# Two decoder blocks on one core: V products of the expert layer with the weights of the tokens stationary, and 128 tokens served by gathering

## The chip, the core and the metric

The kernel runs on one core of a Trainium2 chip, in one launch. The metric is the device time of one execution in microseconds; the kernel before has a median of 2870.73 us over three runs (2870.41 to 2872.3). All arithmetic is in float32: products are made of three float32r matmuls, since every operand is split into a high part and a low rest (high x high, high x low, low x high).

## The reference, cut to what matters

Two decoder layers over 512 tokens of 1024 channels. The change lies in the feed-forward part of the first one, a layer with 16,384 experts of one hidden unit each, of which every token takes 128 (8 heads, 16 each):

```
s = einsum(q, keys)                      # two sets of 128 key scores per head
sv, si = top_k(s, 16); top_s, sel = top_k(sums of pairs, 16)
eidx = the 128 expert numbers of a token; g = softmax(top_s)
u = u_tab[eidx]                          # rows of 1024
act = gelu(einsum('chkd,cd->chk', u, xb))
w = g * act
out = einsum('chk,chkd->cd', w, v_tab[eidx])
```

## The kernel before, in words

Tokens stand in columns: hT is 128 channels by 8 blocks by 528 tokens. The expert layer treats 416 of the 512 tokens **densely** and the other 96 **by gathering**.

Dense: the experts are cut into 128 chunks of 128. For each chunk `u_chunk` (L905) multiplies the U rows of the chunk with the 416 normed tokens (24 matmuls, `mm_late`, L264) and takes gelu; the result, 128 experts by 416 tokens, is `act`. The routing (`routing`, L1119, a generator that is fed from a budget of DVE time per chunk, `BUD`, L47) turns the top-k results into the dense matrix G of gate weights, 128 experts by tokens for each chunk: one-hot rows on DVE (`onehots`), matmuls and a scaled copy (`build_g`, L1105), 16 tokens at a time, 26 blocks, written to a DRAM buffer `gd`. Of the 128 chunks 84 (`ahead`, L189) have their U products made in the U stage, while DVE routes, and are spilled to DRAM (`ad`); the other 44 ("fresh") are made later, between the V products.

V stage (from L1152): in 16 runs of 8 chunks. `load_g` (L1160) reads a run's G back, in 2 transfers from POOL's queue; `load_a` reads a spilled act; `w_prod` (L1172) multiplies act with G on DVE; `w_split` (L1178) makes `wth` and `wtl`. `v_pass` (L1189) is called twice per run, once per half of the channels. It takes 512 of the 1024 columns of the chunk's V rows as the stationary operand, 4 blocks of 128, and the 416 tokens as the moving one, 24 matmuls per chunk over both halves, and sums the 8 chunks of the run in PSUM; then two DVE instructions (L1206) add the sums to hT.

Gathered: `gathered` (L928) is a generator of steps, `gstep` takes one. A step fetches 128 rows of U, or later of V, by expert number (`indirect_dma_start` from POOL's queue, L935) into one of 3 buffers `row` (GB), two steps ahead of its use, and does one DVE multiply over 128 x 1024: U rows with the token and a sum along the row (L949), V rows scaled and added up (L958). Groups (64 tokens, 2 copies) and (32, 4) make 128 + 64 steps. 26 gathers come ahead of the first read of G, the other 166 in the V stage.

Order: everything is in program order on each engine. V rows (`Stream`, L96) are split into high and low by ACT (L119) and DVE (L121), two pieces ahead; U weights of fresh chunks by ACT and POOL. SP issues the loads. `enter` (L1214) splits hT for the next layer and sums its squares; in the last pass its first four blocks are called between the V products of the second half.

Of the kernel before, what the change touches and what calls it, by code (L numbers as in the profile page):

```python
# [46 lines left out]
BUD = 5.0  # L47
# [12 lines left out]
GROUPS = ((64, 2), (32, 4))  # L60
# [32 lines left out]
GV = (1, 2, 4, 6)  # L93
# [48 lines left out]
def _body(tc, nc, V, S, PE, GP, A, out, upto, tap, ctx):  # L142
    def pool(stack, name, bufs=1, **kw):
        if kw.get("space") != bass.MemoryType.DRAM:
# [11 lines left out]
                 "nsa": NSAP}  # L156
# [619 lines left out]
    with ExitStack() as st:  # L776
        with st0 as st1:
            with ExitStack() as st2:
# [59 lines left out]
                xnh, xnl = xtile(xp)  # L838
# [22 lines left out]
                def norm_x(k):  # L861
                    tn = xq.tile([128, T], F32, name="tn", bufs=2)
                    V.scalar_tensor_tensor(tn, H[k], col("g_ffn", k), rB[:, :T], op0=OP.mult, op1=OP.mult)
                    split(xnh[:, k], xnl[:, k], tn, None)
# [40 lines left out]
            def u_chunk(c, p, bufs=3):  # L905
# [3 lines left out]
                a = p.tile([128, TD], F32, name="act", bufs=bufs)  # L909
                S.activation(a, ps, AF.Gelu)  # L910
                return a
# [16 lines left out]
            def gathered():  # L928
# [4 lines left out]
                def load(a, v, j):  # L933
                    g = gx.tile([128, 1024], F32, name="row", bufs=GB)
# [4 lines left out]
                for t in todo[:GB - 1]:  # L939
                    load(*t)  # L940
                yield
# [29 lines left out]
            gat, gac = [], {}  # L971

# [172 lines left out]
            while live:  # L1145
                try:
# [4 lines left out]

        pk = pool(st, "pk")  # L1152
        vs_ = pool(st, "vs", 4)
        order = [f0 + sp_ + f1 for f0, sp_, f1 in runs]
        order[0] = runs[0][0] + runs[0][2] + runs[0][1]
# [4 lines left out]
        def load_g(r):  # L1160
            if r < len(runs):
                gt[r] = pk.tile([128, NSB, RUN, SUB], F32, name="gt", bufs=2)
                for b in range(0, NSB, NSB // GP_):
                    sl = slice(b, b + NSB // GP_)
                    nc.gpsimd.dma_start(gt[r][:, sl].rearrange("p b i t -> p b (i t)"),
                                        gd[sl, :, RUN * r:RUN * (r + 1)].rearrange("b p i t -> p b (i t)"))

        def load_a(c):
            aw[c] = pk.tile([128, TD], F32, name="act", bufs=6)
            nc.sync.dma_start(aw[c], ad[c])  # L1170

        def w_prod(c):  # L1172
            r = c // RUN
            a = aw[c]
            V.tensor_tensor(a.rearrange("p (b t) -> p b t", t=SUB), a.rearrange("p (b t) -> p b t", t=SUB),
                            gt[r][:, :, c % RUN, :], op=OP.mult)

        def w_split(c):  # L1178
            a = aw.pop(c)
            hi = pk.tile([128, TD], F32R, name="wth", bufs=RUN + 2)  # L1180
            lo = pk.tile([128, TD], F32R, name="wtl", bufs=RUN + 2)
# [3 lines left out]
        def u_fresh(c):  # L1185
            aw[c] = u_chunk(c, pk, 6)
            gstep(GU)

        def v_pass(r, h, steps, after=None):  # L1189
            acc = [bank("d") for _ in range(2)]  # L1190
            for j, c in enumerate(order[r]):
                w = vst.get()
                for d in range(4):
                    mm3(acc[d // 2][:, (d % 2) * 512:(d % 2) * 512 + TD], w, d * 128, nw[c][0], nw[c][1],
                        j == 0, j == RUN - 1)
                for fn, arg in steps.get(j, ()):
                    fn(arg)
                if j in GV:
                    gstep()
                if h == 1:  # L1200
                    nw.pop(c)
            for fn, arg in steps.get(RUN, ()):
                fn(arg)
            for d in range(2):
                k = 4 * h + 2 * d
                V.tensor_tensor(hT[:, k:k + 2, M0:M0 + TD], acc[d].rearrange("p (a t) -> p a t", a=2)[:, :, :TD],  # L1206
                                hT[:, k:k + 2, M0:M0 + TD], op=OP.add)
            if after is not None:
                after(range(4 * h, 4 * h + 4))
# [18 lines left out]
        def skew(seq, ahead_):  # L1228

            st_ = {}  # L1230
            for j, c in enumerate(seq):
                if c is not None:
                    st_.setdefault(j - ahead_, []).insert(0, (w_prod, c))
                    st_.setdefault(j - ahead_ + 1, []).append((w_split, c))
            return st_

        load_g(0)
        f0, sp_, f1 = runs[0]
        early = f0 + f1 + runs[1][0][:PRE]
        nf = len(early)  # L1240
        for i, c in enumerate(early):
            if i == nf - EL:
                for c_ in order[0][:2]:
                    w_prod(c_)
                for c_ in order[0][:2]:
                    w_split(c_)
                vst.pump(3, 1)
            u_fresh(c)
            if i == VP:
                vst.pump(3, -1)  # L1250
        for c in sp_[:6 - nf]:
            load_a(c)
        w_prod(order[0][2])
        steps0 = skew([None, None, None] + order[0][3:], 2)
        steps0[0] = [(w_split, order[0][2])]
        for j, c in enumerate(sp_[6 - nf:]):
            steps0.setdefault(j, []).append((load_a, c))
# [647 lines left out]
```

## Time and profile before

| | |
|---|---|
| median of three runs | 2870.73 us |
| profiled execution | 2870.35 us, span 2868.2 us |
| PE, DVE, ACT, POOL busy | 96, 66, 42, 31% of the span |
| U stage (350 to 850.7 us) | PE busy 472.3, DVE 421.8 us |
| V stage (850.7 to 1615 us) | PE busy 760.0, DVE 577.3 us, DMA 284 GB/s |

The profile is of one execution. Stages are told apart by the lines that run in them; a stage's limit is the engine that nobody keeps waiting there. A matmul's own duration in the trace includes its way through the array and overlaps the next, so rates are read from starts.

### The profile page before, as it was taken

The page shows a single profiled execution, that of the slowest core. Times are in us where ns is not written, and L with a number is a line of the kernel's source. Part 1 is how long each engine was busy: PE and PEld are TensorE (multiplying, and loading weights), DVE is VectorE, ACT ScalarE, POOL GpSimd, SP SyncE. Part 2 cuts the span into 40 slices and gives each one's busy share as a digit, 9 for nine tenths or more (in the row PEclk, how much of TensorE's full clock was granted, in tenths as well). Part 3 has the DMA queues.
Part 4 walks back from the last instruction along what each step waited for, and adds up shares of the span by engine and source line. Part 5 has one row for each costly group of instructions (what it writes and reads, how often), then busy time and mean ns, then how long its engine had stood idle before and what let it go on. Part 6 is the DMA issues. An engine that isn't in the chain of part 4 may idle for free. (4 is left out here: it accounts for less than half of the span.)

```text
span 2868.2 us, 38216 instructions
## 1 busy us (share of the span) xinstructions
PE 2758.8 (96%) x14308; PEld 2429.1 (85%) x14308; DVE 1905.4 (66%) x3477; ACT 1193.5 (42%) x1962; POOL 876.0 (31%) x521
## 2 busy tenths in 40 slices
PE   8778998999999999999999999999999999999998
PEld 7646898999989999999999988888887866788887
DVE  5887599798957867777778765444436489544433
ACT  5564543646553333343333423332223378433322
POOL 3653155555534456564456000000003133000000
PEclk9889999999999999999999999999999999999999
DMA  3102255767678888888888333333234200233332
GB/s 126 52 8 66 70 175 179 262 193 259 211 278 305 285 295 281 306 283 280 294 296 301 99 101 96 96 97 100 91 101 141 81 23 1 74 99 100 96 94 83
DMA packets 156568, 457.17 MB, mean 159 GB/s; under 512 B 17056, under 2 KB 40864, under 8 KB 152800
## 3 DMA queue, kind: packets, MB, share of 16 engines
q1 hardware_dynamic: 103008, 273.33, 29.5%
q0 software_dynamic: 36704, 135.54, 14.2%
q10 hardware_dynamic: 16672, 45.88, 4.0%
q8 instruction: 112, 1.84, 0.3%
q14 instruction: 72, 0.59, 0.1%
HBM read 407.43 MB, written 47.25 MB: 159 GB/s over the span
## 5 line engine op out<-in xcount | busy, mean ns | idle before, releaser
L119 ACT CAST wh<-wr 128x1024 fp32r<-128x1024 f32 (+1 forms) x356 | 369.4, 1038 | 394.4 <-issue 206.3
L121 DVE TENSOR_TENSOR wl<-wr,wh 128x1024 fp32r<-128x1024 f32 (+1 forms) x231 | 287.5, 1245 | 368.1 <-ACT wh L119 363.4
L121 POOL TENSOR_TENSOR wl<-wr,wh 128x1024 fp32r<-128x1024 f32 x125 | 334.0, 2673 | 330.2 <-ACT wh L119 325.4
L262 PE MATMUL m<-xh,wl 128*128 128x512 f32 x1080 | 422.2, 391 | 3.4 <-POOL wl L121 2.7
L260 PE MATMUL m<-xh,wh 128*128 128x512 f32 x1080 | 424.4, 393 | 0.0
L261 PE MATMUL m<-xl,wh 128*128 128x512 f32 x1048 | 407.9, 389 | 0.0
L269 PE MATMUL m<-xh,wh 128*128 128x416 f32 x1024 | 365.0, 356 | 9.7 <-ACT stg L1115 5.8
L261 PE MATMUL d<-wtl,vh 128*128 128x416 f32 x1024 | 359.5, 351 | 2.6 <-DVE wtl L253 2.6
L260 PE MATMUL d<-wth,vh 128*128 128x416 f32 x1024 | 359.8, 351 | 1.8 <-DVE hT L1206 0.9
L270 PE MATMUL m<-xl,wh 128*128 128x416 f32 x1024 | 360.9, 352 | 0.0
L262 PE MATMUL d<-wth,vl 128*128 128x416 f32 x1024 | 359.1, 351 | 0.2
L121 DVE TENSOR_TENSOR vl<-vr,vh 128x512 fp32r<-128x512 f32 x256 | 174.7, 688 | 140.1 <-ACT vh L119 133.9
L262 PEld LDWEIGHTS m<-xh,wl 128*128 128x128 f32 x1080 | 203.2, 188 | 49.4 <-DVE wl L121 3.4
L260 PEld LDWEIGHTS m<-xh,wh 128*128 128x128 f32 x1080 | 203.2, 188 | 43.3 <-issue 1.2
L119 ACT CAST vh<-vr 128x512 fp32r<-128x512 f32 x256 | 153.9, 619 | 206.1 <-DMA vr<-in_vr 148.5
L261 PEld LDWEIGHTS m<-xl,wh 128*128 128x128 f32 x1048 | 196.8, 188 | 41.2 <-issue 1.0
L935 POOL DMA_INDIRECT row<-in_vr,gix x96 | 174.6, 1818 | 141.0 <-DVE xt L958 109.3
L272 PE MATMUL m<-xh,wl 128*128 128x416 f32 x1024 | 213.3, 350 | 0.0
L910 ACT ACTIVATE act<-m 128x416 f32<-128x416 f32 x128 | 66.4, 519 | 343.3 <-PE m L272 336.5
L269 PEld LDWEIGHTS m<-xh,wh 128*128 128x128 f32 x1024 | 194.9, 190 | 15.8 <-ACT stg L1115 10.2
L261 PEld LDWEIGHTS d<-wtl,vh 128*128 128x128 f32 x1024 | 192.3, 188 | 5.5 <-DVE wtl L253 3.8
L260 PEld LDWEIGHTS d<-wth,vh 128*128 128x128 f32 x1024 | 192.2, 188 | 5.1 <-ACT act L910 1.3
(428 smaller groups left out, 5378.5 us busy)
## 6 DMA issues: line engine op xcount, KB each, us to landing
wr<-in_u SPq DMA_DIRECT2D x128, 512.0 KB
vr<-in_vr SPq DMA_DIRECT2D x256, 256.0 KB
wr<-in_w_gu SPq DMA_DIRECT2D x88, 512.0 KB
gd<-stg ACTq DMA_DIRECT2D x26, 1024.0 KB
gt<-gd POOLq DMA_DIRECT2D x32, 832.0 KB
ad<-act ACTq DMA_DIRECT2D x84, 208.0 KB
act<-ad SPq DMA_DIRECT2D x84, 208.0 KB
wr<-in_w_down SPq DMA_DIRECT2D x32, 512.0 KB
```

Source lines behind the costliest of these rows:

```text
L119: nc.scalar.copy(hi[:, :n], t[:, :n])
L121: eng.tensor_tensor(lo[:, :n], t[:, :n], hi[:, :n].bitcast(F32), op=OP.subtract)
L260: PE.matmul(ps, lhsT=wh, rhs=xh, start=first, stop=False)
L261: PE.matmul(ps, lhsT=wh, rhs=xl, start=False, stop=False)
L262: PE.matmul(ps, lhsT=wl, rhs=xh, start=False, stop=last)
L269: PE.matmul(ps, lhsT=wh, rhs=xhs[k], start=k == 0, stop=False)
L270: PE.matmul(ps, lhsT=wh, rhs=xls[k], start=False, stop=False)
L272: PE.matmul(ps, lhsT=w[1][:, wc + k * 128:wc + k * 128 + 128], rhs=xhs[k], start=False, stop=k == n - 1)
L910: S.activation(a, ps, AF.Gelu)
L935: GP.indirect_dma_start(out=g, out_offset=None, in_=A["vr" if v else "ur"], in_offset=bass.IndirectOffsetOnAxis(ap=gix[:, a, j:j + 1], axi ...
```

## The change

V products change sides: `wth`/`wtl` (128 experts by 128 tokens) are stationary and the V rows move, 512 columns at a time. The sums, 3 token tiles by 1024 channels, stay in six PSUM banks over all 128 chunks (a new PSUM layout with 2 banks left for the rest). At the end they are copied out, transposed in 128 x 128 blocks and added to hT, and only then is `enter` called. There are no half passes: each chunk's V rows are loaded and split once, whole. 128 tokens are gathered, in two groups of 64, so 384 are dense and G has 24 blocks. In the V stage five gathered tiles are in flight (`rowx`, GX = 2 more buffers). G is read in 6 pieces, after the first run from ACT's queue. Three fresh U chunks stand ahead of the first V product instead of five.

```diff
-BUD = 5.0
+BUD = 4.7
-GROUPS = ((64, 2), (32, 4))
+GROUPS = ((64, 2), (64, 2))
-GV = (1, 2, 4, 6)
+GV = 2
+GX = 2
...
+                 "dense": (("m", 1, 2), ("d", 2, 3))}
...
-                    g = gx.tile([128, 1024], F32, name="row", bufs=GB)
+                    g = None
+                    if gp["pk"] is not None:
+                        if gp["n"] % (GB + GX) < GX:
+                            g = gp["pk"].tile([128, 1024], F32, name="rowx", bufs=GX)
+                        gp["n"] += 1
+                    if g is None:
+                        g = gx.tile([128, 1024], F32, name="row", bufs=GB)
...
-                    if n + GB - 1 < len(todo):
-                        load(*todo[n + GB - 1])
+                    while loaded < min(len(todo), n + gp["la"] + 1):
+                        load(*todo[loaded])
+                        loaded += 1
...
-        vst = Stream(nc, vs_, "vr", vs_, "vh", "vl", [A["vr"][c * 128:c * 128 + 128, h * 512:h * 512 + 512] for o in order for h in range(2) for c in o],
-                     3, 2, 512)
+        vst = Stream(nc, vs_, "vr", vs_, "vh", "vl", [A["vr"][c * 128:c * 128 + 128] for c in seq], 4, 2)
...
-        def v_pass(r, h, steps, after=None):
-            acc = [bank("d") for _ in range(2)]
-            for j, c in enumerate(order[r]):
-                w = vst.get()
-                for d in range(4):
-                    mm3(acc[d // 2][:, (d % 2) * 512:(d % 2) * 512 + TD], w, d * 128, nw[c][0], nw[c][1],
-                        j == 0, j == RUN - 1)
...
+        acc = [bank("d") for _ in range(NT)]
+        def v_pass(c, w):
+            first, last = c == seq[0], c == seq[-1]
+            def part(t, i, j):
+                for h in range(2):
+                    f = slice(h * 512, h * 512 + 512)
+                    PE.matmul(acc[t][:, f], lhsT=nw[c][i][:, t * 128:t * 128 + 128], rhs=w[j][:, f],
+                              start=first and i + j == 0, stop=last and j == 1)
...
+        for n, c in enumerate(seq):
+            w = vst.get()
+            v_pass(c, w)
+            if n + 3 < len(seq) and seq[n + 3] in ad:
+                load_a(seq[n + 3])
+            if n + 2 < len(seq):
+                w_prod(seq[n + 2])
+            if n + 1 < len(seq):
+                w_split(seq[n + 1])
+            gstep(1 + (n % GV == 0))
+            r, j = n // RUN, n % RUN
+            if j < PG // 2:
+                for b in range(2):
+                    load_g(r + 1, 2 * j + b, nc.scalar)
+            for c_ in when.get(n, ()):
+                u_fresh(c_)
...
+        for t in range(NT):
+            y = vs_.tile([128, 1024], F32, name="vr")
+            S.copy(y[:, :512], acc[t][:, :512])
+            V.tensor_copy(y[:, 512:], acc[t][:, 512:])
+            for h in range(2):
+                ps = bank()
+                for k in range(4):
+                    PE.transpose(ps[:, k * 128:k * 128 + 128], y[:, (4 * h + k) * 128:(4 * h + k + 1) * 128], ident)
+                x = hT[:, 4 * h:4 * h + 4, M0 + t * 128:M0 + t * 128 + 128]
+                V.tensor_tensor(x, ps.rearrange("p (k t) -> p k t", k=4), x, op=OP.add)
+        psum_set("gemm")
+        enter(range(4))
+        enter(range(4, 8))
```

PE, the V products about one chunk, before: `d_` are the two sums of a half pass, `vh`/`vl` the split V rows, `wth`/`wtl` the split weights of the tokens; what stands behind the arrow first is the moving operand.

```order
L260 MATMUL d_8184<-wth_8132,vh_8140 128x416
L261 MATMUL d_8184<-wtl_8133,vh_8140 128x416
L262 MATMUL d_8184<-wth_8132,vl_8141 128x416
L260 MATMUL d_8183<-wth_8201,vh_8185 128x416
L261 MATMUL d_8183<-wtl_8202,vh_8185 128x416
L262 MATMUL d_8183<-wth_8201,vl_8186 128x416
```

The same place on PE now, one chunk whole.

```order
L1212 MATMUL d_7864<-vh_7974,wth_8041 128x512 x2
L1212 MATMUL d_7864<-vh_7974,wtl_8042 128x512 x2
L1212 MATMUL d_7865<-vh_7974,wth_8041 128x512 x2
L1212 MATMUL d_7865<-vh_7974,wtl_8042 128x512 x2
L1212 MATMUL d_7866<-vh_7974,wth_8041 128x512 x2
L1212 MATMUL d_7866<-vh_7974,wtl_8042 128x512 x2
L1212 MATMUL d_7864<-vl_7975,wth_8041 128x512 x2
L1212 MATMUL d_7865<-vl_7975,wth_8041 128x512 x2
L1212 MATMUL d_7866<-vl_7975,wth_8041 128x512 x2
```

Eighteen matmuls of 512 columns into three sums take the place of 24 of 416 columns, and the products that need the low part of V come last.

DVE in the second half pass of a run, before: `vl` is the rest of a V split, `act<-act,gt` the product with G, `wtl` the rest of the weights' split, `row` a gathered tile.

```order
L121 TENSOR_TENSOR vl_9369<-vr_9345,vh_9368 128x512
L1175 TENSOR_TENSOR act_9338<-act_9338,gt_9108 128x416
L253 TENSOR_TENSOR wtl_9386<-act_9302,wth_9385 128x416
L949 SCALAR_TENSOR_TENSOR row_9304,gdt_2839<-row_9304,xt_2718 128x1024
L121 TENSOR_TENSOR vl_9397<-vr_9366,vh_9396 128x512
L1175 TENSOR_TENSOR act_9364<-act_9364,gt_9108 128x416
```

DVE in the V stage now, two chunks.

```order
L122 TENSOR_TENSOR vl_9520<-vr_9410,vh_9519 128x1024
L1189 TENSOR_TENSOR act_9471<-act_9471,gt_9161 128x384
L255 TENSOR_TENSOR wtl_9545<-act_9434,wth_9544 128x384
L968 SCALAR_TENSOR_TENSOR xt_9015<-row_9441,gdt_2839,xt_9015 128x1024
L968 SCALAR_TENSOR_TENSOR xt_9015<-rowx_9444,gdt_2839,xt_9015 128x1024
L122 TENSOR_TENSOR vl_9560<-vr_9447,vh_9559 128x1024
L1189 TENSOR_TENSOR act_9541<-act_9541,gt_9161 128x384
L255 TENSOR_TENSOR wtl_9585<-act_9471,wth_9584 128x384
```

A chunk's V split is one instruction, product and split are of neighbouring chunks, and up to two gathered tiles stand between.

PE at the end of the V stage, before: `m_` is the first sum of the next layer, `xh`/`xl` its split input.

```order
L260 MATMUL d_15414<-wth_15237,vh_15539 128x416
L261 MATMUL d_15414<-wtl_15238,vh_15539 128x416
L262 MATMUL d_15414<-wth_15237,vl_15540 128x416
L260 MATMUL m_15622<-xh_15453,wh_15202 128x512
L261 MATMUL m_15622<-xl_15454,wh_15202 128x512
```

The same place now; `vr` are the copied sums.

```order
L1212 MATMUL d_7866<-vl_13955,wth_14000 128x512 x2
L1289 MATMUL m_14041<-ident_94,vr_14038 128x128 x4
L1289 MATMUL m_14047<-ident_94,vr_14038 128x128 x4
L1289 MATMUL m_14056<-ident_94,vr_14053 128x128 x4
L1289 MATMUL m_14062<-ident_94,vr_14053 128x128 x4
L1289 MATMUL m_14071<-ident_94,vr_14068 128x128 x4
L1289 MATMUL m_14077<-ident_94,vr_14068 128x128 x4
L262 MATMUL m_14166<-xh_14093,wh_13861 128x512
```

Twenty-four transposes now lie between the last V product and the next layer's first one.

## Rows read from the trace of the kernel before

**Rows 1.** Part 1 of the page: busy us, share of the span, instructions.

```profile
PE 2758.8 (96%) x14308; PEld 2429.1 (85%) x14308; DVE 1905.4 (66%) x3477; ACT 1193.5 (42%) x1962; POOL 876.0 (31%) x521
```

**Rows 2.** Busy time by stage: U stage, V stage, the layer behind.

```profile
core 0: us, PE busy (x) PEld busy (x) DVE busy (x) ACT busy (x) POOL busy (x), PEclk, DMA share, GB/s
350.00:850.70 500.70, 472.29 (x2995) 456.49 (x2994) 421.81 (x1131) 256.94 (x318) 258.32 (x115) 0.98 0.66 220
850.70:1615.00 764.30, 759.99 (x4036) 751.08 (x4037) 577.30 (x821) 280.00 (x476) 395.97 (x231) 1.00 0.83 284
1615.00:2200.00 585.00, 584.21 (x2573) 479.83 (x2572) 302.28 (x377) 174.82 (x218) 21.84 (x19) 1.00 0.32 100
```

**Rows 3.** Timeline of PE, three stretches: start us, us, engine line op out<-in.

```profile
1179.73 0.35 PE L261 MATMUL d<-wtl,vh 128*128 128x416 f32 x1
...
1191.78 0.35 PE L262 MATMUL d<-wth,vl 128*128 128x416 f32 x1
...
2195.68 0.39 PE L261 MATMUL m<-xl,wh 128*128 128x512 f32 x1
...
2197.95 0.39 PE L262 MATMUL m<-xh,wl 128*128 128x512 f32 x1
...
19.81 0.28 PE L399 MATMUL d<-xl,wh 128*128 128x264 f32 x1
...
21.74 0.28 PE L400 MATMUL d<-xh,wl 128*128 128x264 f32 x1
...
20.05 0.19 PEld L399 LDWEIGHTS d<-xl,wh 128*128 128x128 f32 x1
```

**Rows 4.** Busy time by stretch, columns as in rows 2: end of the routing.

```profile
816.80:829.40 12.60, 8.76 (x74) 7.98 (x75) 5.62 (x5) 10.19 (x12) 0.00 (x0) 0.73 0.86 328
829.40:850.70 21.30, 21.03 (x113) 20.56 (x111) 11.59 (x17) 7.59 (x12) 6.14 (x5) 1.00 0.85 301
```

**Rows 5.** Timeline of ACT and DVE behind the last V product.

```profile
1615.94 2.57 ACT L255 ACTIVATE xh<-hT,gfa 128x512 fp32r<-128x512 f32 x4 [6.06 <-DVE hT L1206]
...
1619.61 4.86 DVE L299 TENSOR_TENSOR nacc<-nacc,sq 128x512 f32<-128x512 f32 x7
```

**Rows 6.** DVE by line, V stage: busy us, mean ns | idle before, releaser.

```profile
L121 DVE TENSOR_TENSOR vl<-vr,vh 128x512 fp32r<-128x512 f32 x256 | 174.7, 688 | 140.1 <-ACT vh L119 133.9 <-issue 2.0 <-DMA vr<-in_vr 1.6
L958 DVE SCALAR_TENSOR_TENSOR xt<-row,gdt,xt 128x1024 f32<-128x1024 f32 x94 | 127.4, 1355 | 6.3 <-DMA row<-in_vr,gix 6.2
...
L949 DVE SCALAR_TENSOR_TENSOR row<-row,xt 128x1024 f32<-128x1024 f32 x68 | 85.2, 1254 | 2.6 <-DMA row<-in_ur,gix 2.6
...
L1206 DVE TENSOR_TENSOR hT<-d,hT 128x832 f32<-128x832 f32 x63 | 61.7, 1016 | 6.9 <-PE d L262 6.6
```

**Rows 7.** POOL by line, V stage, and the timeline of one gather.

```profile
L935 POOL DMA_INDIRECT row<-in_vr,gix x96 | 174.6, 1818 | 141.0 <-DVE xt L958 109.3 <-DMA vr<-in_vr 7.4 <-PE d L262 5.8
L121 POOL TENSOR_TENSOR wl<-wr,wh 128x1024 fp32r<-128x1024 f32 x39 | 108.6, 2784 | 77.0 <-ACT wh L119 72.9 <-issue 4.1
L935 POOL DMA_INDIRECT row<-in_ur,gix x66 | 77.2, 1170 | 122.1 <-DVE row L949 100.4 <-DMA vr<-in_vr 7.3 <-PE d L262 5.8
L1165 POOL DMA_DIRECT2D gt<-gd x30 | 35.6, 1193 | 0.1
...
1182.19 3.76 POOL L935 DMA_INDIRECT row<-in_vr,gix  x1 [0.66 <-DVE xt L958]
...
1185.05 1.28 DVE L958 SCALAR_TENSOR_TENSOR xt<-row,gdt,xt 128x1024 f32<-128x1024 f32 x1
```

**Rows 8.** DMA queues, V stage: packets, MB, share of 16 engines.

```profile
q0 software_dynamic: 30062, 110.52, 43.8%
q1 hardware_dynamic: 54288, 105.78, 39.2%
```

**Rows 9.** Busy time by stretch, columns as in rows 2: two short stretches.

```profile
1110.00:1115.00 5.00, 5.00 (x28) 4.95 (x27) 3.67 (x5) 1.76 (x3) 1.15 (x1) 1.00 1.04 399
1000.00:1020.00 20.00, 20.00 (x108) 19.85 (x107) 13.67 (x21) 5.47 (x10) 6.36 (x6) 1.00 1.01 348
```

More of the change, by code (lines that the diff above doesn't have):

```diff
@@ L1149, in _body @@
                     live = False
+        psum_set("dense")
         pk = pool(st, "pk")
-        vs_ = pool(st, "vs", 4)
-        order = [f0 + sp_ + f1 for f0, sp_, f1 in runs]
-        order[0] = runs[0][0] + runs[0][2] + runs[0][1]
-        vst = Stream(nc, vs_, "vr", vs_, "vh", "vl", [A["vr"][c * 128:c * 128 + 128, h * 512:h * 512 + 512] for o in order for h in range(2) for c in o],
-                     3, 2, 512)
+        vs_ = pool(st, "vs", 3)
+        NT = TD // 128
+        seq = [c for f0, sp_, f1 in runs for c in sp_ + f0 + f1]
@@ L1178, in w_split @@
         def w_split(c):
             a = aw.pop(c)
[L1180 to L1181 removed]
+            hi = pk.tile([128, TD], F32R, name="wth", bufs=3)
+            lo = pk.tile([128, TD], F32R, name="wtl", bufs=3)
             split(hi, lo, a, None)
@@ L1185, in u_fresh @@
         def u_fresh(c):
-            aw[c] = u_chunk(c, pk, 6)
+            aw[c] = u_chunk(c, pk, 4, "fct")
             gstep(GU)
-        def v_pass(r, h, steps, after=None):
-            acc = [bank("d") for _ in range(2)]
-            for j, c in enumerate(order[r]):
-                w = vst.get()
-                for d in range(4):
-                    mm3(acc[d // 2][:, (d % 2) * 512:(d % 2) * 512 + TD], w, d * 128, nw[c][0], nw[c][1],
-                        j == 0, j == RUN - 1)
[L1196 to L1209, printed above, removed]
+        acc = [bank("d") for _ in range(NT)]
[6 more added lines that the diff above has]
+                              start=first and i + j == 0, stop=last and j == 1)
+            if last:
+                for t in range(NT):
+                    for i, j in ((0, 0), (1, 0), (0, 1)):
+                        part(t, i, j)
+            else:
+                for t in range(NT):
+                    part(t, 0, 0)
+                    part(t, 1, 0)
+                for t in range(NT):
+                    part(t, 0, 1)
+            nw.pop(c)
         st9 = {}
@@ L1226, in enter @@
                 st9["n"][1].add(H[k], col("g_final", k))
[L1228 to L1246, printed above, removed]
+        when = {}
@@ new lines, in _body @@
+        for r, (f0, sp_, f1) in enumerate(runs):
+            fr = f0 + f1
+            for n, c in enumerate(fr):
+                when.setdefault(-1 if r == 0 else RUN * r + 2 * n + (-1 if len(fr) > 2 else 0), []).append(c)
+        for b in range(PG):
+            load_g(0, b, nc.gpsimd)
+        for c in seq[:3]:
+            load_a(c)
+        gp["pk"], gp["la"] = pk, GB + GX - 1
+        todo = list(when.pop(-1))
+        for n, c in enumerate(todo):
+            if n == len(todo) - 1:
+                w_prod(seq[0])
+                w_prod(seq[1])
+                w_split(seq[0])
@@ new lines, in _body @@
+        while gat:
+            gstep()
+        st9["w"] = ws.get()
+        for t in range(NT):
+            y = vs_.tile([128, 1024], F32, name="vr")
[7 more added lines that the diff above has]
+                V.tensor_tensor(x, ps.rearrange("p (k t) -> p k t", k=4), x, op=OP.add)
```

65 lines of the change are left out of this document (18 added, 47 removed).

## The prediction

> **What bounds the kernel now.** I read part 1 of the page first, then busy time by stage, then the timeline of single matmuls, then the other engines and the DMA queues of the one stage that changes most. TensorE is busy 96% of the span [rows 1], so the reader should ask in each stage whether it is still the engine that nobody keeps waiting. The stages [rows 2]: the dense U products with the routing (350 to 850.7 us) have PE busy 472 of 501 us and DVE 422; the dense V products (850.7 to 1615) have PE busy 760 of 764 us at full clock, DVE 577, POOL 396, and the DMA engines at 0.83 of their time and 284 GB/s. So the V stage is paid by the matmul; the DMA engines come second, and that is where I look for the next limit.
>
> A busy PE says nothing of how fast it steps; starts do. A 416-column matmul follows the last after 0.188 us (1179.73 to 1191.78 is 64 steps), a 512-column one after 0.227 (10 steps in 2.27 us), a 264-column one after 0.121 (16 steps in 1.93 us) [rows 3]. 384 columns lie between 264 and 416 and come to 0.121 + 120/152 x 0.067 = 0.174; from 416 and 512 downwards 0.188 - 32 x 0.039/96 = 0.175. I take 0.1745. The weight load shown in the same rows takes 0.19 us, longer than the 0.121 between two 264-column matmuls, so it is overlapped there and sets no floor.
>
> The Trainium skill, TensorE: Matmul & The Clock Gate, Back-to-back issue gap, says that the step in a stream of load and matmul pairs is set by both. With a load of 0.19 as the floor the 384-column step would stay at 0.188; the 264-column rows disagree, and this stands below as a rival with a small chance.
>
> **The change part by part.**
> V products: 24 matmuls of 416 columns per chunk of 128 experts become 18 of 512 (3 token tiles, 3 products, 2 halves). 128 x 24 x 0.188 = 578 us become 128 x 18 x 0.227 = 523: -55. All on the path: PE is idle 4 us in the stage.
> U products: 128 x 24 matmuls lose 32 columns each: 3072 x (0.188 - 0.1745) = -41. One third of them stand in the V stage, two thirds in the U stage, where DVE could eat the gain; I charge 4 us there (between 0 and 10: PE waits some 28 us in that stage already, and DVE falls with it, by two blocks of one-hot rows).
> G: 26 blocks become 24, each 32 matmuls on PE. By the row of the last three blocks [rows 4], PE is busy 8.76 us in 12.6 at a clock of 0.73, that is 4.2 us for each where nothing else is there to run, and less than half of it where U products lie between. Two fewer: about -4. But the order shows five blocks in one row behind the last spilled U chunk where there were three; two more at 4.2 - 1.9 = 2.3 is +5.
> Start of the V stage: from the last G evacuation to the first V matmul lie 21.3 us, which five U chunks cover wholly (PE 21.03 busy) [rows 4]. Now three chunks of 24 x 0.1745 = 4.2 us cover 12.6. What they hide is the writing of the last G block, its reading and the first product. The last piece read is now 4 blocks, not 13. Between 0 and 21.3 - 12.6 = 8.7; I take 3.
> End of the V stage: the sums now stand tokens by channels; each token tile is copied out, transposed in 8 pieces and added, and only then can the next layer's input be split. Before, four of the eight splits lay under the last V pass. Nothing runs beside this now. The row shows four ACT splits in 2.57 us and the seven DVE sums of squares in 4.86 [rows 5]; copy, transposes, two adds and the first split of the last tile come to about 4 us, 24 transposes to some 2, and the fifth split stands behind eight squares on ACT, 2 us later than PE wants it: +8 (6 to 12).
> DVE in the V stage: the hT adds go (61.7 us), the splits of V are 128 of 1024 columns instead of 256 of 512, and there are 231 gathered tiles to multiply instead of 164 (94 + 68 and two first ones): 67 x 1.31 = +88 [rows 6]. 577 - 62 + 88, less an estimated 16 for shorter tiles and fewer V splits, is 587 of about 706 us: 83%, still under PE.
> POOL: 32 loads of G at 1.19 us each leave its queue [rows 7] for ACT's, whose engine has casts queued behind them but is busy under 40% of the stage; their wait, a buffer read one run earlier, has long ended. Nothing charged.
> DMA: what must arrive in the V stage is V 128 x 512 KiB, U 41 x 512, gathers 231 x 512, G 24 x 64 KiB x 16 and activations 84 x 192: 251 MB. PE's own time there is 523 + 41 x 4.2 + 12 (what the stage has now beside its products) = 706 us, so it asks for 356 GB/s, where it asked for 284. The queue that carries the gathers moved 110.5 MB in 43.8% of 764 us, 330 GB/s; the other 353 [rows 8]. At these rates the transfers take 121.1/0.330 + 130/0.353 = 735 us, 29 over PE. Against that, stretches with several queues full ran at 399 GB/s over 5 us and 348 over 20 [rows 9]; at 399 it is 630 us and hidden. Five gathered rows in flight instead of three keep the queues full. A gathered row that is late stops DVE, with the next chunk's split behind it, and PE waits for that. From 0 to 29: I take 15.
>
> Sum: -55 - 41 - 4 + 4 + 5 + 3 + 8 + 15 = -65. Against the profiled execution's 2870.35 us (span 2868.2 and 2.1 around it; the median of the runs is 0.4 above, which makes no difference): **2805 us**. Its own range is 2780 (no stall, small edges) to 2835.
>
> **Rivals.**
> A. The DMA engines become the bound of the V stage and the queues are no better fed than now: +29 instead of +15, and the other edges at their upper ends (10, 9, 12) because late rows delay these too: 2870 - 100 + 5 + 29 + 31 = 2835 (2820 to 2860). For it: 356 GB/s asked against 284 at a share of 0.83, which scales to 342. Against it: the 399 in short stretches.
> B. POOL's issuing of gathers becomes the bound, and it ends slower than before. A V-row gather held POOL 3.76 us at 1182.19, which started just behind a DVE multiply and ended 0.9 us into the next one at 1185.05; U rows take 1.17 on average and V rows 1.82 [rows 7]. POOL has per chunk 706/128 = 5.5 us, of which 41/128 x 2.78 = 0.9 goes for splits of U weights; for 1.8 gathers per chunk that leaves 2.6 us each. The price is 128 V-row gathers by what they exceed it: with 3.76 + 0.65 of turnaround for half of them and 1.82 + 0.65 for the rest the mean is 3.4, and 128 x 0.8 = 105 us takes the place of the 15: 2895. It decides from 2.6 + 80/128 = 3.2 us per gather upwards. For it: DVE will run with fewer gaps than now. Against it: a held gather ends with the next multiply, and multiplies now come every 706/231 = 3.1 us with five buffers to spread them.
> The Trainium skill, SBUF — State Buffer, Who interferes with whom, speaks for B: a DVE instruction with two SBUF inputs locks out a GpSimd instruction that reads SBUF, wholly, for its whole length. The 3.76 agrees, the 1.17 of the U rows beside the same DVE work does not.
> C. The change doesn't do what it says for U: 384 columns step like 416, the U gain is lost: 2805 + 41 = 2846.
> D. Edges and stalls each at their worst eat everything: within 0.2% of before.
>
> **How the numbers follow.** Chances: the forecast 0.56, A 0.24, B 0.11, C 0.04, D 0.05. The predicted time is that of the likeliest case. The range for 8 in 10 holds the forecast's own range and A's, and leaves out B and D: 2780 to 2860. 0.2% (6 us) is what a measurement can tell from no change. Faster: 0.56 + 0.24 + 0.04 and a little of D = 0.85; same 0.04; slower 0.11.
>
> **What would show each step.** V matmuls 0.227 us apart and 18 per chunk; U matmuls at 0.174 (0.188 would be C). V stage about 720 us, with idle time on PE put down to DVE (the split of the activations) or ACT, and behind that DVE waiting for gathered rows: a DMA share near 1.0 beside it is A, a POOL busy nearly throughout with V-row gathers above 3 us each is B. A PE gap of some 4 and 2 us at the end of the stage, low clock over five G blocks before it. I am wrong if the V stage is not shorter than 764 us, or if the U stage does not lose about 30 us (9 of them only moved, being two U chunks that now stand in the V stage).

## The result, and the profile after

The changed kernel takes 2800.53 us (median of four runs, 2794.19 to 2801.73) against 2870.57 before: a ratio of 0.9751, 95% interval 0.9734 to 0.9768. The forecast was 2805, from -65 us. The profiled execution has a span of 2799.9 us, 68.3 less than before. Part 1 of its page, columns as in [rows 1]:

```profile
PE 2671.5 (95%) x13497; PEld 2252.2 (80%) x13497; DVE 1958.7 (70%) x3377; ACT 1154.2 (41%) x1827; POOL 931.7 (33%) x559
```

Busy time by stage, columns as in [rows 2]: the U stage of the kernel before; then, of the changed kernel, the U stage, the first 24 us of the V stage, within these the two stretches in which PE works behind a long wait, the middle of the V stage, and 17 us behind the last V product.

```profile
351.90:850.70 498.80, 471.05 (x2988) 455.49 (x2985) 419.91 (x1119) 255.06 (x314) 258.32 (x115) 0.98 0.66 221
```

```profile
353.20:821.30 468.10, 433.16 (x2873) 416.71 (x2870) 402.68 (x1097) 242.33 (x299) 262.56 (x118) 0.97 0.66 222
...
821.30:845.00 23.70, 18.10 (x56) 13.92 (x57) 16.83 (x25) 8.02 (x11) 9.58 (x6) 0.74 1.04 367
821.30:826.50 5.20, 5.20 (x12) 4.14 (x13) 5.20 (x6) 3.54 (x5) 2.26 (x2) 0.50 0.95 317
838.50:843.60 5.10, 5.06 (x12) 3.99 (x13) 5.10 (x8) 0.41 (x2) 2.12 (x2) 0.50 1.13 337
845.00:1525.00 680.00, 678.02 (x3224) 590.02 (x3223) 619.30 (x697) 237.01 (x330) 437.69 (x260) 1.00 0.98 354
1533.00:1550.00 17.00, 13.05 (x57) 9.29 (x56) 14.26 (x23) 11.15 (x19) 0.00 (x0) 0.90 0.04 18
```

The U stage fell from 498.8 us (351.9 to 850.7) to 468.1, the stretch from the first V product to the first product of the next layer from 765.1 to 718.7. In its 680 us in the middle PE idles 2 us although the DMA engines are at 0.98 and DVE at 0.91 of their time. What is idle lies at the two ends. The granted clock there is 0.74 and 0.90, a mean over its two levels, 1.2 and 2.4 GHz; in the two short stretches it is 0.50, the lower level throughout, behind waits of PE of 4.14 and 5.15 us. The kernel before has a clock of 1.00 in the same place, from 850.7 to 880 us.

The steps, from PE's timeline: 18 V matmuls from 1180.40 to 1184.48 are 0.227 us each, 24 U matmuls from there to 1188.66 are 0.174. Both are what the prediction took from [rows 3].

```profile
1180.40 0.62 PE L1212 MATMUL d<-vh,wth 128*128 128x512 f32 x2
...
1184.48 0.34 PE L271 MATMUL m<-xh,wh 128*128 128x384 f32 x1
...
1188.66 0.62 PE L1212 MATMUL d<-vh,wth 128*128 128x512 f32 x2
```

The start of the V stage, from the timelines of PE and DVE. The first product waits 4.14 us for the high part of V, which ACT makes. Then the spilled activation of the fourth chunk is late: DVE's product waits 4.00 us for it, and behind that product stands the split that PE needs for the third chunk, so PE waits 5.15 us.

```profile
821.27 1.22 PE L1212 MATMUL d<-vh,wth 128*128 128x512 f32 x2 [4.14 <-ACT vh L120]
...
837.46 0.56 DVE L1189 TENSOR_TENSOR act<-act,gt 128x384 f32<-128x384 f32 x1 [4.00 <-DMA act<-ad]
...
838.54 1.22 PE L1212 MATMUL d<-vh,wtl 128*128 128x512 f32 x2 [5.15 <-DVE wtl L255]
```

The end, from PE's timeline: behind the last V products (1532.47) come 24 transposes that wait for copies and adds, then the first product that waits for the first split; later one waits for the fifth split, and at 1555.17 one for the sum of squares. [Rows 5] show the same splits and sums of the kernel before, where PE stays fed.

```profile
1532.47 0.62 PE L1212 MATMUL d<-vl,wth 128*128 128x512 f32 x2
1532.93 1.03 PE L1289 MATMUL m<-ident,vr 128*128 128x128 f32 x8
1534.40 0.63 PE L1289 MATMUL m<-ident,vr 128*128 128x128 f32 x4 [0.44 <-DVE hT L1291]
...
1537.70 0.63 PE L1289 MATMUL m<-ident,vr 128*128 128x128 f32 x4 [0.88 <-DVE vr L1285]
1539.94 0.79 PE L262 MATMUL m<-xh,wh 128*128 128x512 f32 x1 [1.61 <-ACT xh L257]
...
1547.63 0.50 PE L262 MATMUL m<-xh,wh 128*128 128x512 f32 x1 [0.18 <-ACT xh L257]
...
1555.17 1.05 PE L310 MATMUL d<-ones,nacc 128*128 128x1 f32 x8 [1.18 <-DVE nacc L301]
```

### The profile page after: what moved, and what is told of

Same layout as the page of the kernel before. It is cut to its first block, busy times and chain, and to the rows that moved or that the text cites. A ratio compares the mean times of both kernels' runs of the same rounds, so it can differ in the third digit from the quotient of the medians.

```text
span 2799.9 us, 36141 instructions
## 1 busy us (share of the span) xinstructions
PE 2671.5 (95%) x13497; PEld 2252.2 (80%) x13497; DVE 1958.7 (70%) x3377; ACT 1154.2 (41%) x1827; POOL 931.7 (33%) x559
## 3 DMA queue, kind: packets, MB, share of 16 engines
q1 hardware_dynamic: 84576, 271.95, 28.7%
## 5 line engine op out<-in xcount | busy, mean ns | idle before, releaser
L271 PE MATMUL m<-xh,wh 128*128 128x384 f32 x1024 | 352.3, 344 | 9.9 <-ACT stg L1127 5.1
L272 PE MATMUL m<-xl,wh 128*128 128x384 f32 x1024 | 347.1, 339 | 0.0
L1212 PE MATMUL d<-vh,wtl 128*128 128x512 f32 x768 | 239.6, 394 | 7.1 <-DVE wtl L255 7.1
L264 PEld LDWEIGHTS m<-xh,wl 128*128 128x128 f32 x1080 | 204.0, 189 | 49.5 <-DVE wl L122 3.4
L1212 PE MATMUL d<-vh,wth 128*128 128x512 f32 x768 | 239.2, 393 | 4.6 <-ACT vh L120 4.1
L263 PEld LDWEIGHTS m<-xl,wh 128*128 128x128 f32 x1048 | 197.7, 189 | 43.3 <-DVE xl L258 1.1
L274 PE MATMUL m<-xh,wl 128*128 128x384 f32 x1024 | 199.6, 336 | 1.0 <-POOL wl L122 0.7
L272 PEld LDWEIGHTS m<-xl,wh 128*128 128x128 f32 x1024 | 195.8, 191 | 1.6
L1212 PE MATMUL d<-vl,wth 128*128 128x512 f32 x768 | 195.6, 390 | 0.0
L122 DVE TENSOR_TENSOR vl<-vr,vh 128x1024 fp32r<-128x1024 f32 x128 | 157.9, 1235 | 52.0 <-ACT vh L120 45.7
L274 PEld LDWEIGHTS m<-xh,wl 128*128 128x128 f32 x1024 | 179.1, 188 | 3.7 <-POOL wl L122 3.6
L1212 PEld LDWEIGHTS d<-vh,wtl 128*128 128x128 f32 x768 | 145.3, 190 | 39.3 <-DVE wtl L255 8.8
```

The lines of the kernel that those rows point to most:

```text
L122: eng.tensor_tensor(lo[:, :n], t[:, :n], hi[:, :n].bitcast(F32), op=OP.subtract)
L263: PE.matmul(ps, lhsT=wh, rhs=xl, start=False, stop=False)
L264: PE.matmul(ps, lhsT=wl, rhs=xh, start=False, stop=last)
L271: PE.matmul(ps, lhsT=wh, rhs=xhs[k], start=k == 0, stop=False)
L272: PE.matmul(ps, lhsT=wh, rhs=xls[k], start=False, stop=False)
L274: PE.matmul(ps, lhsT=w[1][:, wc + k * 128:wc + k * 128 + 128], rhs=xhs[k], start=False, stop=k == n - 1)
```

## The experiments

Every kernel was timed beside the kernel before, on the same chip, and the ratio is that to the kernel before. All but the first start from the changed kernel; its own four runs lie 7.5 us apart, so two variants of it within 5 us are not told apart by their times. Where PE's starts are used, "behind full speed" is what the steps took beyond the steps of a fed PE at 2.4 GHz; it holds waits and low clock alike.

### What the swap is worth: the kernel before with 128 tokens gathered

```diff
-GROUPS = ((64, 2), (32, 4))
+GROUPS = ((64, 2), (64, 2))
-GV = (1, 2, 4, 6)
+GV = (0, 1, 2, 4, 5, 6)
```

> The kernel before with 128 tokens gathered (groups 64 and 64, six steps in each half pass) and nothing else of the change: V rows still stand on the stationary side. Theory (most of the gain is columns, not the swap): V 3072 steps of 0.1735 instead of 0.1895 us give -49, U the same less some 10 eaten in the routing gives -37, two G blocks -3: 2781 if nothing stalls; the DVE then has some 650 us of work in a V stage of 705, with three rows in flight, so 10 to 30 us of stalls: 2790 to 2815. Rival (the swap is needed: without it the 62 us of adds to hT stay on DVE and the rows come late): the V stage stays over 750 us, 2835 or more.

2930.2 us, ratio 1.0201 (1.0184 to 1.0218): about 2% slower than before. The rival holds, and by far more than it said. Its V stage, columns as in [rows 2], two of DVE's groups there (as in [rows 6]), and what PE waited for (us in total, times, longest us):

```profile
825.00:1664.70 839.70, 739.10 (x4040) 723.81 (x4041) 668.22 (x916) 270.46 (x476) 435.62 (x295) 0.95 0.85 295
```

```profile
L958 DVE SCALAR_TENSOR_TENSOR xt<-row,gdt,xt 128x1024 f32<-128x1024 f32 x126 | 177.4, 1408 | 81.0 <-DMA row<-in_vr,gix 80.8
L949 DVE SCALAR_TENSOR_TENSOR row<-row,xt 128x1024 f32<-128x1024 f32 x100 | 133.9, 1339 | 45.4 <-DMA row<-in_ur,gix 45.4
```

```profile
PE d L262 <- DVE vl L121: 60.0, 21, 8.5
...
PE d L260 <- DVE hT L1206: 28.7, 14, 3.1
```

DVE waits 126 us for rows while the engines move 295 GB/s: three rows in flight don't fill them, and a DVE that has 668 us of work has no room to wait. PE in turn waits for DVE's splits and, 28.7 us, for its adds to hT, which the swap does away with.

### Depth alone: three gathered rows in flight

```diff
-GX = 2
+GX = 0
```

> The changed kernel with three gathered rows in flight in the V stage instead of five. Theory (depth is what hides the rows): two steps of 3.1 us ahead are 6.2 us, and a row's flight is 2.7 to 8.3 us with a mean of 6.0, so about half come late by 1 us; DVE waits 50 us or more for rows, PE loses 10 to 40: 2810 to 2840. Rival (the kernel before waited only 9 us for rows with the same three buffers): no change, 2800.

2861.5 us, ratio 0.9961 (0.9947 to 0.9975). The theory's side, but +61 instead of +10 to +40. V stage and the group of DVE:

```profile
821.70:1590.70 769.00, 725.22 (x3322) 609.91 (x3323) 641.33 (x724) 249.97 (x343) 418.19 (x267) 0.99 0.91 324
```

```profile
L968 DVE SCALAR_TENSOR_TENSOR xt<-row,gdt,xt 128x1024 f32<-128x1024 f32 x126 | 176.1, 1398 | 66.3 <-DMA row<-in_vr,gix 65.5
```

In the changed kernel the same group waits 0.6 us. With the run above the V stage, up to the last V product, splits up: 840 us with 128 tokens gathered alone, 769 with the whole change but its depth, 711 with all of it. The swap's matmul steps explain 10 of the first 70 (18 of 0.227 against 24 of 0.1735 us, 128 times). 28.7 are the waits for the adds to hT, which have gone; the rest was not taken apart, since these two kernels also differ in how V rows are split, how G is read and how many fresh chunks stand ahead.

### Columns alone: U products at 416 columns

```diff
-                xnh, xnl = xtile(xp, c=TD)
+                xnh, xnl = xtile(xp, c=416)
...
-                ps = bank()[:, :TD]
+                ps = bank()[:, :416]
```

> The changed kernel with its U matmuls at 416 columns (32 columns are computed and not used). Theory (the U gain is the step, 0.173 against 0.188 us): 3072 x 0.0155 = +47, less the waits in the U stage that it covers (some 10): +37, 2838. Rival (the U stage is set by DVE's routing there, so two thirds of the gain never came): +16 from the V stage alone, 2817.

2823.4 us, ratio 0.9828 (0.9812 to 0.9844): +23, nearer to the rival. Its stages:

```profile
352.00:830.10 478.10, 454.21 (x2872) 439.17 (x2871) 405.02 (x1097) 242.75 (x299) 255.20 (x118) 0.99 0.66 218
830.10:1555.00 724.90, 717.00 (x3322) 621.94 (x3321) 633.36 (x724) 245.16 (x343) 439.36 (x266) 1.00 0.96 344
```

In the U stage PE is busy 21 us longer (its 87 x 24 steps are 32 us longer in sum), and the stage is only 10.0 longer. In the V stage 13.3 of 15 come. So in the changed kernel two thirds of the gain in the U stage are lost. PE idles there 34.9 us instead of 23.9, and its busy time fell by 21 us only, not by 32: its granted clock is 0.97 against 0.99, which by an estimate from these two shares costs it up to 9 us. DVE is busy 403 and 405 us in the two runs, so its routing didn't become shorter with the products. But DVE waits for PE's G products too, so which of the two sets the pace is not shown:

```profile
DVE o L1107 <- PE m L1126: 39.6, 15, 6.1
```

### The DMA engines: no gathers, and no G

```diff
         gp["pk"], gp["la"] = pk, GB + GX - 1
+        gat.clear()
```

> The changed kernel without the gathers of the V stage (their part of the computation is left out): some 116 MB less to move, DVE and POOL half idle. Theory (PE's steps pay the stage, the DMA engines at a share of 0.96 cost nearly nothing): the three waits of 1 us in the middle and part of the start go, -4 to -9: 2792 to 2796. Rival (the DMA engines cost the 15 us that the prediction charged, in stretched steps that no wait shows): -15 or more, 2785 or less.

2781.2 us, ratio 0.9682 (0.9666 to 0.9698): -19, the rival's side in size. Of the 21.9 that its profiled span is shorter 16.4 lie between the first and last V product: 3.4 are the 32 matmuls that fold the gathered sums (L973); the other 13 are waits and low clock, and of these 10 stood in the first 30 us of the stage (1.3 us behind full speed there instead of 11.2). 4.6 lie far behind, in code that is the same, and stay unexplained.

```profile
820.30:1515.70 695.40, 694.61 (x3290) 604.34 (x3291) 367.51 (x386) 245.04 (x341) 97.03 (x39) 1.00 0.56 186
```

So no stretched steps hide in the middle: the price of the gathers is paid where the V stage begins. This run takes away DVE's and POOL's share of them too (DVE is busy 367.5 us instead of 638.7), so it doesn't tell what of the 13 us the DMA engines cost. The next one lightens the DMA engines alone: it reads G for the first two runs only.

```diff
+            if r >= 2:
+                gt[r] = gt[r % 2]
-            if r < len(runs):
+            elif r < len(runs):
```

> The changed kernel with G read for the first two runs only, the others use these again (so the dense sums are wrong from the third run on). 22 MB in 512-byte pieces go, 12% of the DMA engines' time in the stage. Theory (PE's steps pay the stage; with 128 KiB more per chunk the engines were just past their limit, without they are just below it): only the 2.8 us of waits behind the first 30 us go, -2 to -4, 2796 to 2798. Rival (the engines already set the pace in part): -8 or more, 2792 or less.

2797.4 us, ratio 0.9749 (0.9736 to 0.9762), the theory's size, though not told apart from the changed kernel by its time. By the trace, with the engines at 0.89 the V stage is 4 us shorter, and these too come off the first 30 us (7.5 us behind full speed instead of 11.2). So lighter DMA engines give 4 of the 13 us; what the other 9 hang on was not taken apart.

```profile
820.40:1528.00 707.60, 702.46 (x3321) 609.32 (x3322) 635.56 (x724) 244.84 (x343) 445.92 (x266) 1.00 0.89 321
```

### The DMA engines: 128 KiB more per chunk

```diff
+            dx = pk.tile([64, 512], F32, name="dx", bufs=1)
+            nc.sync.dma_start(dx, A["vr"][c * 128:c * 128 + 64, :512])
```

> The changed kernel with 128 KiB more read per chunk of the V stage (64 x 2 KiB of the V rows, into a tile that nobody reads): 16.8 MB more, so that PE's pace asks for 375 GB/s instead of 351. Theory (the DMA engines still have room, up to the 399 GB/s of short stretches, and five rows in flight ride out the rest): 0 to +8, 2800 to 2808. Rival (they are at their limit near 355 GB/s): +16.8 MB / 0.355 = +47, less the few us that they idle now: +35 to +47, 2835 to 2847.

2900.8 us, ratio 1.0098 (1.0082 to 1.0115): +100, twice what even the rival gave. The stage, and what DVE and PE waited for (us in total, times, longest us):

```profile
819.50:1632.00 812.50, 731.88 (x3322) 625.18 (x3323) 637.54 (x724) 247.94 (x343) 437.95 (x266) 0.95 0.99 327
```

```profile
DVE act L1189 <- DMA act<-ad: 89.0, 26, 7.5
...
PE d L1212 <- DVE wtl L255: 78.0, 21, 7.1
```

The queues over 680 us in the middle (845 to 1525 us), of the changed kernel and then of this one (packets, MB, share of 16 engines):

```profile
q0 software_dynamic: 32072, 116.77, 46.3%
q1 hardware_dynamic: 34856, 101.02, 39.4%
```

```profile
q1 hardware_dynamic: 38786, 102.22, 44.3%
q0 software_dynamic: 28376, 103.32, 43.5%
```

With 6.7% more bytes in the stage (265.9 MB for 249.2) the engines are at 0.99 and move 327 GB/s, less than the 350 that they moved between the first and the last V product before: the gathered megabyte holds them 6% longer (43.5 / 103.32 against 46.3 / 116.77), that of SP's queue 11% longer. So the theory, which counted on a reserve up to 399 GB/s, falls.

That the DMA engines alone cost the 100 us is not shown. The extra pieces are 2 KiB instead of 4, and they go into one buffer, so SP issues each only when the one before has landed, with the loads of activations and V rows queued behind it. SP's longest waits in the stage, in this run and then in the changed kernel:

```profile
SPq L1267 <- DMA dx<-in_vr: 381.6, 112, 8.1
```

```profile
SPq L113 <- DVE vl L122: 494.6, 119, 9.2
```

In the changed kernel SP stands because its buffers are still full, that is ahead of need; here it stands for the dose, and activations are what DVE then lacks. Either can make these waits, and no run gave the dose more buffers or another queue. That the changed kernel runs within 2% of where the DMA engines take over is an estimate from their share of 0.98.

### The start of the V stage

```diff
-        gp["pk"], gp["la"] = pk, GB + GX - 1
+        gp["pk"], gp["la"] = pk, GB - 1
...
+            if n == 6:
+                gp["la"] = GB + GX - 1
```

> The changed kernel with three gathered rows in flight over the first seven chunks of the V stage and five from then on. Theory (the five rows issued at once stand ahead of the first activations and V rows, and cost 10 of the 13 us that go when no rows are gathered): the 5.5 us wait at the fourth chunk and the low clock behind it go, -6 to -9: 2792 to 2795. Rival (with three in flight the rows themselves come late at the start, as they did in the run with three throughout): within 3 us of the changed kernel.

2796.6 us, ratio 0.9740 (0.9724 to 0.9756): not told apart from the changed kernel, and its start waits as before (5.87 us between two starts of PE in the third chunk, which the fourth chunk's activation holds up). The theory of a burst of five rows falls. The waits there, columns as above:

```profile
ACT vh L120 <- DMA vr<-in_vr: 9.4, 2, 6.2
DVE act L1189 <- DMA act<-ad: 4.3, 1, 4.3
```

```diff
-        for c in seq[:3]:
+        for c in seq[:4]:
             load_a(c)
...
-            if j < PG // 2:
+            if 2 <= j < 2 + PG // 2:
                 for b in range(2):
-                    load_g(r + 1, 2 * j + b, nc.scalar)
+                    load_g(r + 1, 2 * (j - 2) + b, nc.scalar)
```

> The changed kernel with the fourth activation read ahead of the V stage and the G of the second run read two chunks later. Theory (the 5.5 us wait at the fourth chunk is one activation behind V rows in SP's queue): it goes, -3 to -6, 2795 to 2797. Rival (the DMA engines are full in these 30 us, and V rows are what is late next; the run with three rows at the start kept its 5.9 us wait): within 2 us.

2832.8 us, ratio 0.9864 (0.9849 to 0.9879): +32, which neither side had. Its first 24 us are mended (21.54 us of PE instead of 18.10 in about the same stretch; which of the two edits does it is not told apart), but G now comes late in run after run:

```profile
821.00:845.00 24.00, 21.54 (x85) 17.02 (x86) 23.02 (x35) 11.05 (x15) 11.88 (x8) 0.93 0.99 352
```

```profile
DVE act L1189 <- DMA gt<-gd: 33.9, 5, 10.6
```

Between the last issue of G and its first use lie two chunks, some 11 us, instead of four. With the engines this full that is too little: a read of G is worth nothing unless it stands early.

### The routing's budget

```diff
-BUD = 4.7
+BUD = 5.0
```

> The changed kernel with the budget of the routing back at 5.0 us per chunk. Theory (DVE sets the U stage, a larger budget only moves the waits from the end of the stage into it): within 4 us, 2796 to 2804. Rival (the five blocks of G left behind the last spilled chunk are what costs: with 5.0 there are three or four again, at 2.3 us each): -4 to -8, with the last blocks of G earlier.

2792.6 us (2789.16 to 2799.91), ratio 0.9732 (0.9714 to 0.9750): the rival's side, though the interval overlaps that of the changed kernel. U stage:

```profile
353.00:815.70 462.70, 429.41 (x2872) 411.45 (x2870) 405.95 (x1098) 242.28 (x300) 266.59 (x120) 0.99 0.67 226
```

5.4 us shorter. Two G blocks now stand in one row instead of five, with four U chunks behind them instead of three; the gain is about the +5 which the prediction charged for the longer row, though the granted clock of the stage is 0.99 here instead of 0.97 too. In its profiled run the V stage is 5.7 shorter as well, with a start that waits 4 us less.

### POOL and DVE

```diff
-        if n >= len(ahead) + PF or n < len(ahead) and n % 6 in PA:
+        if n < len(ahead) and n % 6 in PA:
```

> The changed kernel with the split of the fresh U weights in the V stage on DVE instead of POOL. Beside 38 of the 39 POOL splits one DVE instruction takes 3.9 instead of 1.2 us, so DVE does 39 x (2.7 - 1.2) = 58 us less in sum. Theory (DVE's waits are hidden behind PE): within 3 us, 2797 to 2803. Rival (these waits make the few late splits in the middle, 2.5 us, and part of the start): -4 or more.

2796.3 us, ratio 0.9734 (0.9718 to 0.9750): the same within what can be told. DVE, which now makes the splits of the fresh U weights, is busy 45 us less, POOL 114 us less, and the stage is what it was: first this kernel, then the changed one over the same stretch.

```profile
820.00:1532.70 712.70, 704.00 (x3322) 610.22 (x3323) 593.43 (x763) 246.00 (x343) 333.13 (x227) 0.99 0.97 350
```

```profile
821.30:1533.00 711.70, 704.12 (x3321) 610.82 (x3322) 638.65 (x724) 246.21 (x343) 447.27 (x266) 0.99 0.97 350
```

### The end of the V stage, and all together

```diff
             if last:
                 for t in range(NT):
                     for i, j in ((0, 0), (1, 0), (0, 1)):
                         part(t, i, j)
+                    ys.append(vs_.tile([128, 1024], F32, name="vr"))
+                    S.copy(ys[t][:, :512], acc[t][:, :512])
+                    (S.copy if t < NT - 1 else V.tensor_copy)(ys[t][:, 512:], acc[t][:, 512:])
+                    if t:
+                        turn(t - 1, ys[t - 1])
+                turn(NT - 1, ys[NT - 1])
...
             for k in ks:
                 split(st9["x"][0][:, k], st9["x"][1][:, k], H[k], st9["g"][:, k:k + 1])
+            if ks[-1] < 7:
+                return
-            for k in ks:
+            for k in range(8):
                 st9["n"][0].add(H[k])
                 st9["n"][1].add(H[k], col("g_final", k))
```

> The changed kernel with another end of the V stage: each token tile is copied out and transposed behind the next tile's products, and the eight splits of the next layer's input come ahead of the sums of squares. Theory (the 7.2 us without a product and some 6 us of late splits and low clock behind them are a chain of short steps, not work): copy 0.7, transposes 0.9, two adds 1.3 and a split 0.65 remain, -4, and the second half of the splits is no longer behind eight squares, -3: -7, 2793. Rival (the squares moved back are late for the norms, and the time is only moved): within 3 us of the changed kernel.

`turn` transposes a tile and adds it to hT. 2798.5 us, ratio 0.9748 (0.9735 to 0.9762): the rival. The first product comes 4.7 us behind the last V product instead of 7.2, the wait for the fifth split has gone, and the sums of squares take it back:

```profile
1539.21 0.49 PE L262 MATMUL m<-xh,wh 128*128 128x512 f32 x1 [1.00 <-ACT xh L257]
...
1554.52 1.65 PE L310 MATMUL d<-ones,nacc 128*128 128x1 f32 x8 [3.51 <-DVE nacc L301]
```

The next layer's 120th product starts 38.3 + 4.7 = 43.0 us behind its last V product, in the changed kernel 36.6 + 7.2 = 43.9, in the kernel before 30.6 + 0.2. (The first number moves by itself: with the changed kernel's own end it lies between 35.1 and 38.3 in the other runs.) What sets this stretch is, as far as these rows go, the chain of splits and squares on ACT and DVE, half of which lay under the last V pass before, and the low clock behind its waits.

The two edits at the ends and the budget together:

> Both of these edits and the budget of 5.0 us together. Theory (they lie at different places and add up): -7 -4 -8 = -19, 2782. Rival (the budget's gain and the start's are the same waits): -10, 2790.

2831.9 us, ratio 0.9872 (0.9857 to 0.9887). The late G decides here as it did in the run with the start's edits: DVE waits 29.2 us for it and the V stage is 749 us long, while the budget's 4 us in the U stage (463.9) are there. No version here is clearly better than the changed kernel; the budget of 5.0 is the one that may be.

## Why the prediction held, term by term

Profiled executions, us; "measured" is worked out from PE's starts in the two traces and the runs above.

| term | predicted | measured |
|---|---|---|
| V products | -55 | -56: 2304 steps of 0.227 for 3072 of 0.188 |
| U columns, less what DVE eats | -37 | -23: 13.3 in the V stage, 10.0 in the U stage (run at 416 columns) |
| G and routing, two blocks fewer and five in a row | +1 | -16: what is left of the U stage's 30.7, beside 9 moved and the wait below; its cause is open |
| V stage, start | +3 | +10: 4 before the first product, 6 in the 30 us behind it (11.2 us behind full speed for 5.3 before) |
| DMA, late rows | +15 | +2 in the rest of the stage (2.7 us behind full speed for 0.9) |
| V stage, end | +8 | +13: 7.0 before the next layer's first product, 6.0 in its first 120 |
| outside of what changed | 0 | +3, as it also differs among runs of the same code |
| sum | -65 | -67, and the span fell by 68.3 |

**V products and U columns: the steps were right**, 0.227 and 0.174, and rival C is out (PE's weight load takes 0.19 in these rows too, and sets no floor).

**U stage: the step that failed is "I charge 4 us there".** The bound was 0 to 10; the run at 416 columns shows that 22 of 32 us of shorter products are lost, half of them as waits of PE, half as a smaller fall of its busy time, with a lower clock. Against it stands a gain of about 16 us that the sum didn't have. DVE's busy time in the stage fell by 17 us (419.9 to 402.7), but two one-hot blocks fewer explain little of that: the four one-hot lines fell from 156.3 to 151.9 us. Another 6.5 us are three gathered U rows that moved into the V stage, first before, then now:

```profile
L949 DVE SCALAR_TENSOR_TENSOR row<-row,xt 128x1024 f32<-128x1024 f32 x28 | 47.8, 1708 | 5.4 <-DMA row<-in_ur,gix 5.4
```

```profile
L959 DVE SCALAR_TENSOR_TENSOR row<-row,xt 128x1024 f32<-128x1024 f32 x25 | 41.3, 1651 | 0.0
```

No run took these apart, so the cause of the gain stays open. Both errors have nearly the same size and opposite sign: that the stage came out at -30.7 where about -30 was said is luck. The price of the row of five G blocks was right: they take 21.0 us (783.35 to 804.38), 4.2 each as said, where one alone between U products takes 2.2.

**DMA and the start: "I take 15" failed, and the start's 3 was too small.** 15 and 3 make 18, and 12 were measured, but in another place and by another mechanism. There are no late rows: DVE waits 0.6 us for V rows in the whole stage. What is lost comes before the first product and in the 30 us behind it, when V rows, U weights, the first G, the second G, activations and rows all want the engines. And the 6 us more than before in these 30 are not longer waits: 5.1 of the 11.2 are the two stretches at 1.2 GHz behind PE's waits, where the matmuls start 0.43 us apart instead of 0.227 (18 take 6.70 us from 821.27, 16 take 6.13 from 838.54). The sum had no term for the clock at either end of the stage. That five rows in flight "keep the queues full" is shown by the run with three: without them some 10 us of the gain of 70 are left. DVE's 587 us in the stage came out at 638.7: its 229 gathered multiplies took 1.57 us each instead of 1.31, mostly for the reason in the last section.

**Rival A was closer than its 0.24 looks.** Its ground (356 GB/s asked, 0.83 scaling to 342) was nearly the whole truth: the engines are at 0.98 in the middle, and moved 354 GB/s. They could just deliver. Its argument against, 399 GB/s in short stretches, was no reserve that the kernel could draw on: with 7% more bytes the engines moved less. How much of the 100 us that this cost is theirs is open, as said above.

**Rival B did not come.** Its bound was 3.2 us for a gather with 0.65 of turnaround. POOL's gathers take 1.55 us for V rows and 1.52 for U rows, with the 0.65 some 2.2, and none in the V stage took longer than 2.61; in the kernel before 18 of 162 took 3.75 or 3.76, all of them V rows:

```profile
L943 POOL DMA_INDIRECT row<-in_vr,gix x77 | 119.4, 1551 | 80.2 <-DVE xt L968 62.1 <-issue 10.2 <-DVE row L959 4.5
...
L943 POOL DMA_INDIRECT row<-in_ur,gix x59 | 89.9, 1524 | 74.5 <-DVE row L959 64.6 <-issue 7.3 <-DVE xt L968 2.5
```

POOL waits for free buffers, not the other way. The Trainium skill, SBUF — State Buffer, Who interferes with whom, has a DVE instruction with two SBUF inputs contend with a GpSimd instruction that reads SBUF, and not with one that only writes it. It also infers that descriptor generation needs the write side, by which a gather would not be held and the page would not speak for B. With DVE at 0.91 of its time this trace has no 3.76, which agrees with that. What held the 18 before stays open.

**The end** cost 13, just over the upper bound of 12. "The fifth split" was seen; two things were not. One is the sums of squares, which the next layer's norm waits for (1.18 us of PE at 1555.17). The other is the clock: behind the first product and again behind the sums PE steps at 1.2 GHz, where the kernel before has 1.00 from 1615.8 to 1655 us. Behind each of the two some 8 products start 0.43 us apart instead of 0.227, an estimated 3 of the 6 us. The second of these stretches, columns as in [rows 2]:

```profile
1557.10:1560.40 3.30, 3.30 (x9) 2.63 (x9) 1.85 (x7) 1.91 (x4) 0.00 (x0) 0.50 0.50 158
```

## What to carry to other kernels

When a stage has one engine at 99%, one at 0.83 and one at 75%, shortening the first brings the others to the front at once: ask of each how far it reaches, and test it with a dose of load. Here 7% more bytes cost 100 us; give such a dose buffers and a queue of its own, or it also tests the order of the loads behind it. Count the clock too: each of the two long waits at the start here left a stretch at 1.2 GHz behind it. Depth of prefetch and the time of another engine are worth as much as the steps saved, so an edit that frees both should be timed with each undone. Reads that are always early enough must stay early: moving one closer to its use to ease a start costs every later round.

## What was not expected of the hardware

A DVE instruction with both inputs in SBUF mostly did not run beside a POOL subtraction of 128x1024. In the changed kernel 33 of the 39 POOL splits of the V stage have one DVE instruction beside them that takes 2.65 us longer (the 38 of the expectation counted overlaps without a delay). In five others the multiply had begun 0.8 us ahead and took its 1.28 us, and the split took 2.75 us instead of 2.40. From the timeline of both:

```profile
922.58 3.93 DVE L959 SCALAR_TENSOR_TENSOR rowx<-rowx,xt 128x1024 f32<-128x1024 f32 x1
923.02 2.39 POOL L122 TENSOR_TENSOR wl<-wr,wh 128x1024 fp32r<-128x1024 f32 x1
...
926.44 1.22 DVE L959 SCALAR_TENSOR_TENSOR row<-row,xt 128x1024 f32<-128x1024 f32 x1
```

The first multiply began 0.44 us ahead of the split and ended 1.1 behind it; the next one took 1.22. Some 87 of DVE's 639 us are such waiting; without it the 39 splits that moved to DVE, at 1.22 us each, would leave it busy about 40 us less, and 45 were measured. The Trainium skill, SBUF — State Buffer, Who interferes with whom, states that two such instructions contend. Here the trace agrees, with 3.93 against 1.22 us, and the gathers, which POOL also issues, are not held in that way.
